# A batched matrix product fed by one stream of DMAs: larger stores, a first load in four pieces, and one loop for all pairs

## The chip, the cores and the metric

The kernel runs on one core of a Trainium2 chip. The metric is the device time of one execution in microseconds (us). The core has five engines that run their own instruction queues and meet at semaphores: TensorE (PE in the profile; its weight loads are PEld) multiplies matrices, VectorE (DVE), ScalarE (ACT) and GpSimd (POOL) work element by element, and SyncE (SP) here does nothing but issue DMAs. Sixteen DMA engines move the data between the memory of the chip (HBM) and the on-chip memory of 128 partitions (SBUF). TensorE writes its results to a small memory of its own (PSUM), from which they have to be copied out.

## The reference

```python
batch, m, k, n = 16, 512, 512, 512
a = np.random.randn(batch, k, m).astype(np.float32)
b = np.random.randn(batch, k, n).astype(np.float32)

def reference(a, b):
    return np.matmul(a.transpose(0, 2, 1), b).astype(np.float32)
```

Sixteen products of 512 x 512 matrices, with a given transposed. Each of a, b and the result is 16.78 MB, so 33.55 MB are read and 16.78 MB written.

## The kernel before

**Pairs of batches.** The batches are taken two at a time, which gives eight pairs. A tile `x` of 128 partitions holds one operand of one pair: batch 0 of the pair lies on partitions 0 to 63 and batch 1 on 64 to 127 (`in_v`, line 34). Each partition has R = 8 successive rows of the matrix, 8 x 2 KB = 16 KB that lie together in HBM. There are four such tiles, `x0` to `x3` (NX = 4), so two pairs fit. Loads are numbered n = 0 to 15: even ones are of a, odd ones of b, and load n goes to tile n % 4.

**The two halves of a pair.** VectorE casts float32 to bfloat16 in two halves of RV = 4 rows (v = 0 and 1), into `abf` and `bbf`, of which there is one tile for each half. TensorE takes half v once both of its casts are there (`s_cast`). One matmul covers the 64 partitions of one batch (g = 0 or 1); the two batches of a pair take turns in the instruction order (lines 140 to 161), each with its own PSUM tiles. The results of a pair add up over both halves; a pair takes 64 matmuls, 32 for each half. ScalarE copies the finished PSUM tiles to the output tile `o` of that pair, in four copies (line 176), and then says so on `s_out` (line 181). There are NO = 7 output tiles for eight pairs, so the last pair reuses that of pair 0 and ScalarE first waits until the store of pair 0 has landed (`s_o0`, line 165).

**The first pair is different.** Its two batches are loaded one after the other, each spread over all 128 partitions (`in0_v`, line 37): a of batch 0, b of batch 0, a of batch 1, b of batch 1, four DMAs of 1 MB with 8 KB for each partition (lines 70 to 73, semaphores `s_f` and `s_x`). VectorE casts them in lines 89 to 98, TensorE has a loop of its own for them with matmuls of the full 128 rows (lines 123 to 139), and ScalarE copies batch by batch (lines 166 to 172). VectorE casts batch 1 into the same tiles as batch 0, so it waits for the matmuls of batch 0 (line 91).

**The queue of DMAs.** SyncE issues everything in one order. From load 4 on it waits until VectorE has cast the tile that is to be overwritten (`s_in`, line 76, counted up by the small memsets of lines 98 and 119). The last load comes in two halves (lines 81 and 82, `s_h`). When the first half of that last load has landed (line 84), SyncE issues the stores, one DMA of 2 MB for each pair, each after its `s_out` (lines 85 to 87). In a store each partition writes 8 KB to each of two batches. So nearly all loads come before all stores in the queue. The store of the last pair stands at the very end, after a barrier (line 188), and GpSimd waits for the other stores (lines 184 to 186).

**Order of the casts.** VectorE's casts of pair i wait for TensorE: half 0 for the matmuls of half 0 of the pair before (`s_v`, line 104; for pair 1 all matmuls of the first pair, line 102), half 1 for all matmuls of the pair before (`s_mm`, line 106). Each also waits for its load (line 112).

Of the kernel before, what the change touches and what calls it, by code (L numbers as in the profile page):

```python
# [8 lines left out]
def kernel(  # L9
# [6 lines left out]
    nc = tc.nc  # L16
    P = 128
    batch, K, M = a.shape
    _, _, N = b.shape
    f32 = mybir.dt.float32  # L20
# [5 lines left out]
    G = 2  # L26
    Q = P // G
    R = K // Q
    V = 2
    RV = R // V  # L30
    T = M // P
    H = T // 2
    pairs = batch // G
    in_v = [x.rearrange("(pair g) (q r) m -> pair (g q) r m", g=G, r=R) for x in (a, b)]


    in0_v = [x.rearrange("batch (p r) m -> batch p r m", r=RV) for x in (a, b)]
    out_v = out.rearrange("(pair g) (c t) n -> pair c g t n", g=G, t=T)

    NX = 4  # L40
    NO = pairs - 1
# [3 lines left out]
    pool = ctx.enter_context(tc.tile_pool(name="sb", bufs=1))  # L45
# [4 lines left out]
    dve_done, act_done = done[:, 0:2 * pairs], done[:, 2 * pairs:3 * pairs]  # L50
    x_ts = [pool.tile([P, R, M], f32, name=f"x{j}") for j in range(NX)]
    abf_ts = [pool.tile([P, RV, M], bf, name=f"abf{v}") for v in range(V)]
    bbf_ts = [pool.tile([P, RV, N], bf, name=f"bbf{v}") for v in range(V)]
    o_ts = [pool.tile([P, G, T, N], f32, name=f"o{j}") for j in range(NO)]
    ps_ts = [[psum.tile([P, 2, N], f32, name=f"ps{g}{h}") for h in range(H)] for g in range(G)]

    s_x = [tc.alloc_semaphore(f"s_x{j}") for j in range(NX)]
    s_f = [tc.alloc_semaphore(f"s_f{j}") for j in range(2)]
    s_h = tc.alloc_semaphore("s_h")
    s_o0 = tc.alloc_semaphore("s_o0")  # L60
    s_o = tc.alloc_semaphore("s_o")
    s_in = tc.alloc_semaphore("s_in")
    s_cast = tc.alloc_semaphore("s_cast")
    s_v = tc.alloc_semaphore("s_v")
    s_mm = tc.alloc_semaphore("s_mm")
    s_ev = [tc.alloc_semaphore(f"s_ev{h}") for h in range(H)]
    s_out = tc.alloc_semaphore("s_out")

    with tc.tile_critical(no_gpsimd_drain=True):  # L69
        for j in range(2):  # L70
            nc.sync.dma_start(x_ts[j][:, 0:RV, :], in0_v[j][0]).then_inc(s_f[j], 16)  # L71
        for j in range(2):
            nc.sync.dma_start(x_ts[j][:, RV:R, :], in0_v[j][1]).then_inc(s_x[j], 16)  # L73
        for n in range(2, 2 * pairs):
            if n >= NX:
                nc.sync.wait_ge(s_in, n - NX + 1)
            src, x = in_v[n % 2][n // 2], x_ts[n % NX]
            if n < 2 * pairs - 1:
                nc.sync.dma_start(x[:], src).then_inc(s_x[n % NX], 16)  # L79
            else:  # L80
                nc.sync.dma_start(x[:, 0:RV, :], src[:, 0:RV, :]).then_inc(s_h, 16)
                nc.sync.dma_start(x[:, RV:R, :], src[:, RV:R, :]).then_inc(s_x[n % NX], 16)

        nc.sync.wait_ge(s_h, 16)
        for i in range(pairs - 1):
            nc.sync.wait_ge(s_out, i + 1)
            nc.sync.dma_start(out_v[i], o_ts[i % NO][:]).then_inc(s_o if i else s_o0, 16)

        for u in range(G):
            if u:  # L90
                nc.vector.wait_ge(s_mm, H)
            for j, bf_ts in enumerate((abf_ts, bbf_ts)):
                nc.vector.wait_ge(s_x[j] if u else s_f[j], 16)
                nc.vector.tensor_copy(  # L94
                    out=bf_ts[0][:], in_=x_ts[j][:, u * RV:(u + 1) * RV, :]
                ).then_inc(s_cast, 1)
                if u == G - 1:
                    nc.vector.memset(dve_done[:, j:j + 1], 0.0).then_inc(s_in, 1)  # L98
        for i in range(1, pairs):
            for v in range(V):  # L100
                if i == 1 and v == 0:
                    nc.vector.wait_ge(s_mm, G * H)
                if i > 1 and v == 0:
                    nc.vector.wait_ge(s_v, G * (i - 1))
                if i > 1 and v == 1:
                    nc.vector.wait_ge(s_mm, G * H * i)
                for n in (2 * i, 2 * i + 1):
                    last = n == 2 * pairs - 1
                    if last and v == 0:
                        nc.vector.wait_ge(s_h, 16)  # L110
                    if last and v == 1 or not last and v == 0:
                        nc.vector.wait_ge(s_x[n % NX], 16 * (n // NX + 1))
                    nc.vector.tensor_copy(  # L113
                        out=(bbf_ts if n % 2 else abf_ts)[v][:],
                        in_=x_ts[n % NX][:, v * RV:(v + 1) * RV, :],
                    ).then_inc(s_cast, 1)
                    if v == V - 1:

                        nc.vector.memset(dve_done[:, n:n + 1], 0.0).then_inc(s_in, 1)  # L119

        for h in range(H):
            nc.tensor.sem_inc(s_ev[h], 1)
        with nc.tensor.Fori(0, G):
            a_m = abf_ts[0][:].rearrange("p r (c t) -> p r t c", t=T)
            nc.tensor.wait_ge(s_cast, 2).then_inc(s_cast, -2)
            for t in range(T):
                h = t // 2
                if t % 2 == 0:
                    nc.tensor.wait_ge(s_ev[h], 1).then_inc(s_ev[h], -1)  # L129
                for r in range(RV):  # L130
                    mm = nc.tensor.matmul(  # L131
                        ps_ts[0][h][:, t % 2, :],
                        a_m[:, r, t],
                        bbf_ts[0][:, r, :],
                        start=(r == 0),
                        stop=(r == RV - 1),
                    )
                if t % 2:
                    mm.then_inc(s_mm, 1)
        with nc.tensor.Fori(0, pairs - 1):  # L140
            for v in range(V):
                nc.tensor.wait_ge(s_cast, 2).then_inc(s_cast, -2)
                for t in range(T):
                    h = t // 2
                    if v == 0 and t % 2 == 0:
                        nc.tensor.wait_ge(s_ev[h], 1).then_inc(s_ev[h], -1)  # L146
                    for r in range(RV):
                        for g in range(G):
                            rows = slice(g * Q, (g + 1) * Q)
                            a_m = abf_ts[v][rows, r, :].rearrange("p (c t) -> p t c", t=T)  # L150
                            mm = nc.tensor.matmul(  # L151
                                ps_ts[g][h][:, t % 2, :],
                                a_m[:, t],
                                bbf_ts[v][rows, r, :],
                                start=(v == 0 and r == 0),
                                stop=(v == V - 1 and r == RV - 1),
                            )
                            if v == 0 and t == T - 1 and r == RV - 1:
                                mm.then_inc(s_v, 1)
                            if v == V - 1 and t % 2 and r == RV - 1:  # L160
                                mm.then_inc(s_mm, 1)

        for i in range(pairs):
            if i == NO:
                nc.scalar.wait_ge(s_o0, 16)
            if i == 0:
                for g in range(G):
                    for h in range(H):
                        nc.scalar.wait_ge(s_mm, H * g + h + 1)
                        nc.scalar.copy(  # L170
                            out=o_ts[0][:, g, 2 * h:2 * h + 2, :], in_=ps_ts[0][h][:]
                        ).then_inc(s_ev[h], 1)
            for h in range(H if i else 0):
                for g in range(G):
                    nc.scalar.wait_ge(s_mm, G * H * i + G * h + g + 1)
                    ev = nc.scalar.copy(  # L176
                        out=o_ts[i % NO][:, g, 2 * h:2 * h + 2, :], in_=ps_ts[g][h][:]
                    )
                ev.then_inc(s_ev[h], 1)

            nc.scalar.memzero(act_done[:, i:i + 1]).then_inc(s_out, 1)  # L181


    with tc.tile_critical(sync_engine=mybir.EngineType.Pool, no_gpsimd_drain=True):
        nc.gpsimd.wait_ge(s_o0, 16)
        nc.gpsimd.wait_ge(s_o, 16 * (pairs - 2))
    tc.no_sync_barrier()
    nc.sync.dma_start(out_v[pairs - 1], o_ts[(pairs - 1) % NO][:])


# [28 lines left out]
```

## Time and profile before

| | |
|---|---|
| median of 10 runs | 123.24 us |
| lowest and highest run | 123.15 and 123.48 us |
| the profiled execution | 123.17 us |
| its span in the profile | 121.4 us |
| instructions | 1207 |
| PE busy | 61.7 us, 51% of the span |
| PEld busy | 34.9 us, 29% |
| DVE busy | 38.1 us, 31% |
| ACT busy | 32.1 us, 26% |
| moved by DMA | 50.33 MB, 415 GB/s over the span |

The span goes from the first to the last instruction of the profile; the remaining 1.8 us of the profiled execution lie around it. All times of single instructions below come from this one execution and are counted from the start of the span. The DMA share is the mean busy share of the 16 DMA engines; it can go a little over 1, since packets are booked where they start and successive ones overlap slightly. "SPq" is the time that an issue of a DMA takes on SyncE's queue, not the transfer itself. A line of the timeline gives the start, the duration, the engine, the line of the kernel, the operation with its tiles, and in brackets how long the engine had been idle and what ended that.

### The profile page before, as it was taken

How to read it: one execution, taken by the hardware profiler on the slowest of the kernel's cores; microseconds unless marked ns; L12 is line 12 of the kernel's file. 1: busy time of each engine (PE TensorE's matmuls, PEld its weight loads, DVE VectorE, ACT ScalarE, POOL GpSimd, SP SyncE). 2: the span in 40 equal slices, each digit the busy share in tenths (PEclk: the TensorE clock that was granted, in tenths of full speed). 3: DMA queues.
4: the chain of work that ended last, by engine and by line, in shares of the span. 5: the costliest groups of instructions: out<-in, count | busy, mean ns of one | idle time of the engine just before them, and what ended most of it. 6: DMA issues, size and time to landing. Idle time of an engine off the chain costs nothing.

```text
span 121.4 us, 1207 instructions
## 1 busy us (share of the span) xinstructions
PE 61.7 (51%) x480; PEld 34.9 (29%) x480; DVE 38.1 (31%) x48; ACT 32.1 (26%) x41; POOL 0.2 (0%) x4
## 2 busy tenths in 40 slices
PE   0007919099379959739979919989900000000000
PEld 0002314066135536424636606655400000000000
DVE  0061070864290394083465447492000000000000
ACT  4000323301900570740092380191560000000000
POOL 0000000000000000000000000000000000000000
PEclk9999999999959999985999999999995555555555
DMA  2999999999999999999999999999999999999994
GB/s 70 429 424 426 443 432 432 432 432 432 432 432 432 432 432 426 426 432 432 432 432 432 432 432 418 426 429 426 426 432 432 424 426 432 424 432 421 429 426 192
DMA packets 4912, 50.33 MB, mean 415 GB/s; under 512 B 432, under 2 KB 432, under 8 KB 432
## 3 DMA queue, kind: packets, MB, share of 16 engines
q1 hardware_dynamic: 4912, 50.33, 97.6%
HBM read 33.55 MB, written 16.78 MB: 415 GB/s over the span
## 4 chain that ended last, share of the span: by engine, by line
DMA 59%; DVE 6%; issue 3%; ACT 3%; SPq 2%; ACTq 0%
DMA x<-in_b_dram 53%; DMA out_dram<-o 6%; ACT o L176 3%; DVE bbf L113 3%; DVE abf L113 3%; SPq L73 1%; SPq L71 1%; SPq L79 0%; DVE done L119 0%; ACTq L69 0%; SPq L214 0%; SPq L69 0%
## 5 line engine op out<-in xcount | busy, mean ns | idle before, releaser
L151 PE MATMUL ps<-bbf,abf 64*128 64x512 bf16 x448 | 52.8, 393 | 13.6 <-PEq L146 13.6
L151 PEld LDWEIGHTS ps<-bbf,abf 64*128 64x128 bf16 x448 | 31.2, 112 | 35.2 <-issue 20.5
L176 ACT COPY o<-ps 128x1024 f32<-128x1024 f32 x28 | 26.3, 1027 | 40.9 <-PE ps L151 36.9
L113 DVE CAST abf<-x 128x2048 bf16<-128x2048 f32 x14 | 17.1, 1224 | 17.4 <-PE ps L151 13.4
L113 DVE CAST bbf<-x 128x2048 bf16<-128x2048 f32 x14 | 17.1, 1225 | 14.6 <-DMA x<-in_b_dram 14.6
L131 PE MATMUL ps<-bbf,abf 128*128 128x512 bf16 x32 | 8.8, 438 | 12.5 <-PEq L129 12.5
L131 PEld LDWEIGHTS ps<-bbf,abf 128*128 128x128 bf16 x32 | 3.7, 121 | 17.1 <-issue 15.1
L170 ACT COPY o<-ps 128x1024 f32<-128x1024 f32 x4 | 4.0, 1012 | 16.1 <-PE ps L131 16.1
L94 DVE CAST abf<-x 128x2048 bf16<-128x2048 f32 x2 | 2.5, 1228 | 11.4 <-DMA x<-in_a_dram 5.8
L94 DVE CAST bbf<-x 128x2048 bf16<-128x2048 f32 x2 | 2.4, 1224 | 1.2 <-DMA x<-in_b_dram 1.2
L181 ACT ACTIVATE done<-done 1x1 uint32<-1x1 uint32 x8 | 1.6, 196 | 0.0
L170 ACT ACT_TABLE_LOAD x1 | 1.3, 1283 | 0.9 <-SPq L69 0.9
L119 DVE MEMSET done<- 1x1 f32 x14 | 0.8, 59 | 0.0
L98 DVE MEMSET done<- 1x1 f32 x2 | 0.1, 59 | 0.0
L203 POOL MEMSET const-bfloat16-1.0<- 128x1 bf16 x1 | 0.1, 101 | 0.0
L203 POOL MEMSET const-uint8-127<- 128x1 uint8 x1 | 0.1, 101 | 0.0
L203 POOL MEMSET const-float32-0.0<- 128x1 f32 x1 | 0.1, 98 | 0.2 <-issue 0.2
L203 POOL MEMSET const-float32-1.0<- 128x1 f32 x1 | 0.1, 98 | 0.0
## 6 DMA issues: line engine op xcount, KB each, us to landing
out_dram<-o SPq DMA_DIRECT2D x8, 2048.0 KB, 21.9
x<-in_a_dram SPq DMA_DIRECT2D x7, 2048.0 KB, 12.2
x<-in_b_dram SPq DMA_DIRECT2D x6, 2048.0 KB, 15.9
x<-in_b_dram SPq DMA_DIRECT2D x4, 1024.0 KB, 12.1
x<-in_a_dram SPq DMA_DIRECT2D x2, 1024.0 KB, 6.8
```

The lines of the kernel that those rows point to most:

```text
L71: nc.sync.dma_start(x_ts[j][:, 0:RV, :], in0_v[j][0]).then_inc(s_f[j], 16)
L73: nc.sync.dma_start(x_ts[j][:, RV:R, :], in0_v[j][1]).then_inc(s_x[j], 16)
L94: nc.vector.tensor_copy(out=bf_ts[0][:], in_=x_ts[j][:, u * RV:(u + 1) * RV, :]).then_inc(s_cast, 1)
L98: nc.vector.memset(dve_done[:, j:j + 1], 0.0).then_inc(s_in, 1)
L113: nc.vector.tensor_copy(out=(bbf_ts if n % 2 else abf_ts)[v][:], in_=x_ts[n % NX][:, v * RV:(v + 1) * RV, :],).then_inc(s_cast, 1)
L119: nc.vector.memset(dve_done[:, n:n + 1], 0.0).then_inc(s_in, 1)
L131: mm = nc.tensor.matmul(ps_ts[0][h][:, t % 2, :], a_m[:, r, t], bbf_ts[0][:, r, :], start=(r == 0), stop=(r == RV - 1),)
L151: mm = nc.tensor.matmul(ps_ts[g][h][:, t % 2, :], a_m[:, t], bbf_ts[v][rows, r, :], start=(v == 0 and r == 0), stop=(v == V - 1 and r == R ...
L170: nc.scalar.copy(out=o_ts[0][:, g, 2 * h:2 * h + 2, :], in_=ps_ts[0][h][:]).then_inc(s_ev[h], 1)
L176: ev = nc.scalar.copy(out=o_ts[i % NO][:, g, 2 * h:2 * h + 2, :], in_=ps_ts[g][h][:])
L181: nc.scalar.memzero(act_done[:, i:i + 1]).then_inc(s_out, 1)
L203: nc = _bacc.Bacc("TRN2", target_bir_lowering=False, num_devices=1)
```

## The change

**Loads.** All pairs now have the layout of `in_v`: two batches side by side on 64 partitions each, in runs of 16 KB for a partition. The separate layout of the first pair goes. The very first load, a of pair 0, is issued in four DMAs: row 0, row 1, rows 2 and 3, rows 4 to 7 of each partition, which are 2, 2, 4 and 8 KB for a partition. The first three count up one semaphore (`s_h[0]`), for which VectorE waits with 48. The load of b of pair 0 is one DMA of 2 MB. The last load keeps its two halves.

**Compute.** The first pair goes through the same casts, the same TensorE loop and the same copies as the others; its own code on VectorE, TensorE and ScalarE goes. The cast of half 0 of pair 1 now waits for `s_v` like that of the later pairs.

**Stores.** The seven output tiles become slices of one tile `o_t`, so that one DMA can take two of them. The first seven pairs are stored in four DMAs: pairs 0 and 1, 2 and 3, 4 and 5 with 4 MB each, and pair 6 with 2 MB. A store waits until both of its pairs are copied. ScalarE's wait for the output tile of pair 0 is therefore a wait for the store of pairs 0 and 1. The store of the last pair is as it was.

```diff
-    in0_v = [x.rearrange("batch (p r) m -> batch p r m", r=RV) for x in (a, b)]
-    out_v = out.rearrange("(pair g) (c t) n -> pair c g t n", g=G, t=T)
+    out_v = out.rearrange("batch (c t) n -> c batch t n", t=T)
...
-    o_ts = [pool.tile([P, G, T, N], f32, name=f"o{j}") for j in range(NO)]
+    o_t = pool.tile([P, NO, G, T, N], f32, name="o")
+    o_ts = [o_t[:, j] for j in range(NO)]
...
-    s_f = [tc.alloc_semaphore(f"s_f{j}") for j in range(2)]
-    s_h = tc.alloc_semaphore("s_h")
+    s_h = [tc.alloc_semaphore(f"s_h{j}") for j in range(2)]
...
-        for j in range(2):
-            nc.sync.dma_start(x_ts[j][:, 0:RV, :], in0_v[j][0]).then_inc(s_f[j], 16)
-        for j in range(2):
-            nc.sync.dma_start(x_ts[j][:, RV:R, :], in0_v[j][1]).then_inc(s_x[j], 16)
-        for n in range(2, 2 * pairs):
+        for n in range(2 * pairs):
             if n >= NX:
                 nc.sync.wait_ge(s_in, n - NX + 1)
-            src, x = in_v[n % 2][n // 2], x_ts[n % NX]
-            if n < 2 * pairs - 1:
-                nc.sync.dma_start(x[:], src).then_inc(s_x[n % NX], 16)
-            else:
-                nc.sync.dma_start(x[:, 0:RV, :], src[:, 0:RV, :]).then_inc(s_h, 16)
-                nc.sync.dma_start(x[:, RV:R, :], src[:, RV:R, :]).then_inc(s_x[n % NX], 16)
+            cuts = (0, 1, 2, RV, R) if n == 0 else (0, RV, R) if n == 2 * pairs - 1 else (0, R)
+            for r0, r1 in zip(cuts, cuts[1:]):
+                done_sem = s_x[n % NX] if r1 == R else s_h[n > 0]
+                nc.sync.dma_start(
+                    x_ts[n % NX][:, r0:r1, :], in_v[n % 2][n // 2][:, r0:r1, :]
+                ).then_inc(done_sem, 16)
 
-        nc.sync.wait_ge(s_h, 16)
-        for i in range(pairs - 1):
-            nc.sync.wait_ge(s_out, i + 1)
-            nc.sync.dma_start(out_v[i], o_ts[i % NO][:]).then_inc(s_o if i else s_o0, 16)
+        nc.sync.wait_ge(s_h[1], 16)
+        for i in range(0, NO, 2):
+            n = min(2, NO - i)
+            nc.sync.wait_ge(s_out, i + n)
+            nc.sync.dma_start(
+                out_v[:, G * i:G * (i + n)],
+                o_t[:, i:i + n].rearrange("p i g t n -> p (i g) t n"),
+            ).then_inc(s_o if i else s_o0, 16)
 
-        for u in range(G):
-            if u:
-                nc.vector.wait_ge(s_mm, H)
-            for j, bf_ts in enumerate((abf_ts, bbf_ts)):
-                nc.vector.wait_ge(s_x[j] if u else s_f[j], 16)
-                nc.vector.tensor_copy(
-                    out=bf_ts[0][:], in_=x_ts[j][:, u * RV:(u + 1) * RV, :]
-                ).then_inc(s_cast, 1)
-                if u == G - 1:
-                    nc.vector.memset(dve_done[:, j:j + 1], 0.0).then_inc(s_in, 1)
-        for i in range(1, pairs):
+        for i in range(pairs):
             for v in range(V):
-                if i == 1 and v == 0:
-                    nc.vector.wait_ge(s_mm, G * H)
-                if i > 1 and v == 0:
-                    nc.vector.wait_ge(s_v, G * (i - 1))
-                if i > 1 and v == 1:
+                if i and v == 0:
+                    nc.vector.wait_ge(s_v, G * i)
+                if i and v == 1:
                     nc.vector.wait_ge(s_mm, G * H * i)
                 for n in (2 * i, 2 * i + 1):
-                    last = n == 2 * pairs - 1
-                    if last and v == 0:
-                        nc.vector.wait_ge(s_h, 16)
-                    if last and v == 1 or not last and v == 0:
+                    split = n in (0, 2 * pairs - 1)
+                    if split and v == 0:
+                        nc.vector.wait_ge(s_h[n > 0], 16 if n else 48)
+                    if split == (v == 1):
                         nc.vector.wait_ge(s_x[n % NX], 16 * (n // NX + 1))
...
-        with nc.tensor.Fori(0, G):
-            a_m = abf_ts[0][:].rearrange("p r (c t) -> p r t c", t=T)
...
-        with nc.tensor.Fori(0, pairs - 1):
+        with nc.tensor.Fori(0, pairs):
...
-            if i == 0:
-                for g in range(G):
-                    for h in range(H):
-                        nc.scalar.wait_ge(s_mm, H * g + h + 1)
-                        nc.scalar.copy(
-                            out=o_ts[0][:, g, 2 * h:2 * h + 2, :], in_=ps_ts[0][h][:]
-                        ).then_inc(s_ev[h], 1)
-            for h in range(H if i else 0):
+            for h in range(H):
...
-        nc.gpsimd.wait_ge(s_o, 16 * (pairs - 2))
+        nc.gpsimd.wait_ge(s_o, 16 * ((NO + 1) // 2 - 1))
     tc.no_sync_barrier()
-    nc.sync.dma_start(out_v[pairs - 1], o_ts[(pairs - 1) % NO][:])
+    nc.sync.dma_start(out_v[:, batch - G:batch], o_ts[(pairs - 1) % NO])
```

More of the change, by code (lines that the diff above doesn't have):

```diff
@@ L122 @@
             nc.tensor.sem_inc(s_ev[h], 1)
-        with nc.tensor.Fori(0, G):
-            a_m = abf_ts[0][:].rearrange("p r (c t) -> p r t c", t=T)
[L125 to L139, printed above, removed]
-        with nc.tensor.Fori(0, pairs - 1):
+        with nc.tensor.Fori(0, pairs):
             for v in range(V):
```

## The prediction

> **What bounds the kernel now.** I read the slice rows of the page first, then its DMA queues, then the table of busy time by stage, then the chain of waits and the timeline. The slice rows and the queue row:
>
> ```profile
> PE   0007919099379959739979919989900000000000
> DMA  2999999999999999999999999999999999999994
> GB/s 70 429 424 426 443 432 432 432 432 432 432 432 432 432 432 426 426 432 432 432 432 432 432 432 418 426 429 426 426 432 432 424 426 432 424 432 421 429 426 192
> q1 hardware_dynamic: 4912, 50.33, 97.6%
> ```
>
> The DMA engines are busy in every slice but the first and the last; TensorE (PE) has whole slices of nothing, and none from slice 30 on. So the program is one stream of 50.33 MB through 16 DMA engines: 33.55 MB of loads, then 16.78 MB of stores. Three things can change its time: the time per row moved, a hole in the stream, and its two ends. The stages, in the busy time by stage (the last two columns are the DMA share and GB/s):
>
> ```profile
> 1.80:2.00 0.20, 0.00 (x0) 0.00 (x0) 0.00 (x0) 0.20 (x1) 0.00 (x0) 1.00 0.54 205
> 2.00:2.20 0.20, 0.00 (x0) 0.00 (x0) 0.00 (x0) 0.18 (x1) 0.00 (x0) 1.00 0.31 123
> 2.20:2.40 0.20, 0.00 (x0) 0.00 (x0) 0.00 (x0) 0.00 (x0) 0.00 (x0) 1.00 1.66 328
> 2.40:2.60 0.20, 0.00 (x0) 0.00 (x0) 0.00 (x0) 0.00 (x0) 0.00 (x0) 1.00 0.00 0
> 2.60:2.80 0.20, 0.00 (x0) 0.00 (x0) 0.00 (x0) 0.00 (x0) 0.00 (x0) 1.00 0.80 205
> 2.80:3.00 0.20, 0.00 (x0) 0.00 (x0) 0.00 (x0) 0.00 (x0) 0.00 (x0) 1.00 0.62 205
> ...
> 20.00:72.00 52.00, 39.82 (x327) 22.98 (x324) 25.37 (x32) 20.33 (x27) 0.00 (x0) 0.93 1.01 433
> ...
> 92.00:118.00 26.00, 0.00 (x0) 0.00 (x0) 0.00 (x0) 0.00 (x0) 0.00 (x0) 0.50 1.01 429
> ```
>
> Loads of 16 KB rows run at 433 GB/s, stores of 8 KB rows at 429, both at a DMA share of 1.01: no hole to fill. Only the ramp is loose: bytes start at 1.8 us, and no packet starts from 2.4 to 2.6. From 1.8 to 3.4 (3.0 to 3.4 shows 369 and 410) the rates times 0.2 us give 369 KB where 430 GB/s would give 688: 0.74 us lost. The issues on the SyncE queue (SPq) at the start and at the change from loads to stores, and the waits that tie the other engines to the stream:
>
> ```profile
> 0.94 0.39 SPq L71 DMA_DIRECT2D x<-in_a_dram  x1
> 1.39 0.42 SPq L71 DMA_DIRECT2D x<-in_b_dram  x1
> 1.86 0.42 SPq L73 DMA_DIRECT2D x<-in_a_dram  x1
> 2.33 0.72 SPq L73 DMA_DIRECT2D x<-in_b_dram  x1
> ...
> 22.86 1.23 DVE L113 CAST bbf<-x 128x2048 bf16<-128x2048 f32 x1 [0.29 <-DMA x<-in_b_dram]
> ...
> 25.28 0.33 SPq L79 DMA_DIRECT2D x<-in_a_dram  x1
> ```
>
> ```profile
> 78.80 7.41 DMA out_dram<-o
> 86.23 3.76 ACT o L176 x4
> ```
>
> An issue takes some 0.42 us, the fourth 0.72. The second pair's last load has landed at 22.86, and the load into the first pair's buffer of a (load 6, counted from 0) is issued at 25.28 once that buffer is cast. The first store is asked for at 78.80, when half of the last load (1 MB, 2.4 us) is still to come, and lands 7.41 us later; ScalarE (ACT) waits for it, copies the last pair out in 3.76 us, and the last store joins a queue that is busy to 120 us. The page's chain gives DMA 59% and no engine more than 6%.
>
> **What the Trainium skill says.** "DMA: Bandwidth & Descriptors", section "Anatomy of one DMA — SWDGE (gpsimd) path": the semaphore write at the end of a DMA costs about one cycle, and most of the fixed 2 us of a DMA is completion latency. It is stated for another issue path than SyncE's, but the trace agrees as far as it goes: 2 MB stores queued behind each other keep 429 GB/s, so a boundary between queued DMAs costs nothing visible, and fewer of them win nothing. The same page, "Latency and other measured facts", puts the first byte of such a DMA at about 600 ns; here the first bytes appear between 1.8 and 2.0, 0.5 to 0.7 us after the first issue ends at 1.33. It also warns that HBM rows at a large power-of-two pitch slow DMAs down; the stores here already step 1 MB from batch to batch at 429 GB/s, so the trace shows no such loss. "SBUF — State Buffer", section "The DMA setup-cost knee (why "@ 1 MiB" ≠ asymptote)", has a 256 KiB transfer at 224 GB/s alone; that is a bound for the small first pieces if they do not overlap, and no row of this trace shows such a size.
>
> **The change, part by part.**
>
> 1. *Price of a row.* 16 engines at 433 GB/s give 605 ns per 16 KB row, at 429 they give 305.5 ns per 8 KB row. Twice the second less the first: about 5.6 ns per row whatever its length (3 to 9, as the rates are whole GB/s), and 37.5 ns per KB. A 2 KB row then costs 80.6 ns, a 4 KB row 155.5 ns: estimates from these two rates.
>
> 2. *First load in four.* Each engine has 8 of the 128 partitions. The first half of a was 8 rows of 8 KB; it becomes 8 of 2, 8 of 2 and 8 of 4 KB: 16 more rows, 16 x 5.6 = +0.09 us. The second half stays at 8 KB.
>
> 3. *b of the first pair.* Two DMAs of 8 KB rows become one of 16 KB rows: 8 rows fewer per engine, -0.045 us.
>
> 4. *Stores.* Seven DMAs become four (two pairs, two, two, one) beside the last, with the same 8 KB rows; loads go from 19 to 20 DMAs, so 27 become 25: two completion writes fewer per engine, between 0 and 0.01 us, taken as 0.
>
> 5. *Hand-over between the small pieces.* A 256 KB piece gives an engine 8 x 80.6 = 0.645 us of work. SyncE issues every 0.45 us, fast enough. But the descriptors come at a slower rate: the fourth issue was held to 0.72 us, and the stores of 256 rows took a median of 1.30 us each, 0.65 us per 128 rows. So the next piece arrives 0 to 0.08 us after the last is used up, twice: I take 0.02 each, +0.04 us. If the stall at 2.4 us stays it gives the descriptors time to get ahead and even this goes. Bounds: below, the shorter rows take the stall away, -0.74 us at the very most; above, each restart costs a new start. At the page's 224 GB/s, 256 KB takes 1.17 us in place of 0.61, so 0.56 us each, +1.1 us at most.
>
> 6. *Later start of the compute.* The first matmul needs half of a and all of b: 4 MB (4.19 million bytes) landed, 9.69 us at 433 before the 22.86 of the 8 MB mark: 13.2 us, and matmuls at 14.7 (24.39 less 9.69) in place of 9.77. Lines 94, 131 and 170 go; the first pair now takes the path of the others, with 64 half-height matmuls. A pair takes 7.1 us (24.39 to 31.49), plus 1.6 us while the clock is cold (16 matmuls took 5.21 us first, 3.62 then): done at 23.4, against 24.01, when the second half of the next pair's a is cast. Load 4 waits for the second cast of a: 25.28 - 9.69 = 15.6 us, earlier than the 16.30 of before, with 4 MB still queued until 22.9. Load 6 is issued at about 25.3 as now, and the queue has work until 32.5. VectorE's new wait for the first half of TensorE's loop is met at 14.7 + 3.6 + 1.6 = 19.9, before that cast's 21.34 of now. Cost 0; the cover is 7 us of queued loads. From the second pair on everything follows the landings, which are the same.
>
> 7. *Stores of 4 MB and the last pair.* ACT's wait for the first store ends 4.9 us later, at 91.1; copies to 94.9; last store asked for at 95.1. The stores before it occupy the engines to about 115 (120.0 less 4.9). Cover 20 us, cost 0. SyncE's waits for two evictions per store come last for pair 6, alone in the fourth store: its copies start at 78.45 and take 3.76, so 82.3, while 12 MB of earlier stores keep the engines busy.
>
> 8. *First 4 MB store.* It has 512 rows to describe, 2.6 us at 0.65 per 128, and 2.4 us of load as cover. The start of the kernel shows that engines begin on the first descriptors while the others are made: starts at 1.8 to 2.0, and the rest at 2.2 to 2.4. So half of the engines get work early, the other half after some 2.0 us (1.0 us for the first 64 rows, as at the start, and three more lots of 64 at 0.32): 80.8 against 81.2. Cost 0. If nothing starts before all 512 are made, it is 1.0 + 7 x 0.32 = 3.3 us, 82.1: a hole of 0.85 us.
>
> 9. *Tail.* The last store has the same 256 rows and its wait is as before: 0.
>
> Sum: 0.09 - 0.045 + 0.04 = +0.085 us. The profiled execution took 123.17 us itself (span 121.4 and 1.8 around it), 0.07 below the median; 123.17 + 0.085 = 123.26 there, 123.32 on the median of 123.24. I forecast 123.3.
>
> **Rivals.**
>
> *Faster:* small first rows shorten the ramp. For it: the empty 0.2 us at 2.4, and the trouble lies where 8 KB rows of all engines begin together. Against: it comes 0.5 us after the first bytes on all engines at once, as if it were not a matter of row length. Half of the 0.74 us, after the +0.045 of rows: 122.9.
>
> *Slower, first pieces:* the engines run dry at the two hand-overs and start again, as in 5. It decides from 0.13 us of hole each (0.25 in all). For it: 0.645 us of work against 0.65 of descriptors leaves no reserve. Against: the stall gives one. With 0.25 each, half of the bound: 123.24 + 0.045 + 0.5 = 123.8.
>
> *Slower, first big store:* part 8's hole, 123.3 + 0.85 = 124.1 at worst, deciding from 0.25. Against: the stepped start at 1.8 us.
>
> *Slower, store rate:* four batches at 1 MB pitch in one DMA run 1% below 429 GB/s: 34 us of stores, +0.34, 123.65. Against: each engine still writes 8 KB rows one after another, as now.
>
> That the change does not do what it says is no rival: the orders of the two programs show the four first loads and the four stores.
>
> **How the numbers follow.** This kernel's measurement tells 0.2% (0.25 us) from no change at best. Forecast, within that: 0.50. Faster 0.17. First pieces 0.19, big store 0.09, rate and anything else 0.05: slower 0.33. Range 122.8 to 124.1: it takes in the faster case, the pieces and the hole of part 8; the likeliest case alone lies in 123.1 to 123.5.
>
> **What would show it.** Right: DMA packets 4912 + 16 x (16 - 8 - 2) = 5008, share of 1.01 at 433 and 429 GB/s in the same stages, matmuls from about 14.7, load 4 at about 15.6, last store asked for near 95, span 121.3 to 121.7. Wrong: under 369 KB moved between 1.8 and 3.4 us (pieces), or well over it (faster); a share under 0.95 between 81 and 83 (big store); under 427 GB/s from 92 to 118 (rate); a load issued when the queue has run dry before 35 us (part 6).

## The result and the profile after

The changed kernel takes 124.95 us (median of 9 runs, 124.47 to 125.89) against 123.24: a ratio of 1.0139, 95% interval 1.0124 to 1.0154. It is slower by 1.7 us, and outside the forecast's range of 122.8 to 124.1. The profiled execution took 124.46 us with a span of 122.5 us, which is 1.29 us and 1.1 us over those of the kernel before, so the traces show most of the loss, and some later runs lost more.

First the slice rows and the queue row of the page of the changed kernel:

```profile
DMA  2999999999999999999999999999999999999993
GB/s 82 310 448 428 417 428 433 433 428 439 428 428 439 433 444 433 433 433 428 428 428 428 428 433 415 415 428 428 428 425 431 428 431 425 431 428 428 425 431 147
DMA packets 5008, 50.33 MB, mean 411 GB/s; under 512 B 400, under 2 KB 400, under 8 KB 784
q1 hardware_dynamic: 5008, 50.33, 97.3%
```

The packets are the 5008 that were counted out in the forecast, and from the third slice on the rates are close to those of before (415 to 448 GB/s up to the last slice, 418 to 443 before). The second slice (3.1 to 6.1 us) shows 310 GB/s, where before had 429. The DMA row alone hides it: its digit is 9 in both. The busy time by stage of the changed kernel (the last two columns are the DMA share and GB/s):

```profile
1.80:3.00 1.20, 0.00 (x0) 0.00 (x0) 0.00 (x0) 0.38 (x1) 0.00 (x0) 1.00 0.67 203
3.00:4.00 1.00, 0.00 (x0) 0.00 (x0) 0.00 (x0) 0.00 (x0) 0.00 (x0) 1.00 0.78 250
4.00:5.00 1.00, 0.00 (x0) 0.00 (x0) 0.00 (x0) 0.00 (x0) 0.00 (x0) 1.00 1.00 307
5.00:6.00 1.00, 0.00 (x0) 0.00 (x0) 0.00 (x0) 0.00 (x0) 0.00 (x0) 1.00 1.06 334
...
20.00:34.00 14.00, 12.53 (x110) 7.12 (x106) 6.30 (x8) 6.65 (x9) 0.00 (x0) 1.00 1.01 431
...
40.00:60.00 20.00, 16.23 (x137) 9.15 (x134) 9.66 (x13) 7.64 (x10) 0.00 (x0) 0.91 1.01 433
100.00:118.00 18.00, 0.00 (x0) 0.00 (x0) 0.00 (x0) 0.00 (x0) 0.00 (x0) 0.50 1.01 427
...
120.00:121.00 1.00, 0.00 (x0) 0.00 (x0) 0.00 (x0) 0.00 (x0) 0.00 (x0) 0.50 0.49 205
```

The same four stages of the kernel before:

```profile
1.80:3.00 1.20, 0.00 (x0) 0.00 (x0) 0.00 (x0) 0.38 (x1) 0.00 (x0) 1.00 0.65 177
3.00:4.00 1.00, 0.00 (x0) 0.00 (x0) 0.00 (x0) 0.00 (x0) 0.00 (x0) 1.00 0.96 401
4.00:5.00 1.00, 0.00 (x0) 0.00 (x0) 0.00 (x0) 0.00 (x0) 0.00 (x0) 1.00 1.01 426
5.00:6.00 1.00, 0.00 (x0) 0.00 (x0) 0.18 (x1) 0.00 (x0) 0.00 (x0) 1.00 1.04 434
```

From 1.8 to 6.0 us the changed kernel moves 1.2 x 203 + 250 + 307 + 334 = 1135 KB, the kernel before 1473 KB by the same sum. The 338 KB less are 0.79 us at 430 GB/s. Two things are to be seen. From 3 to 4 us the DMA share is 0.78: engines stand idle. From 4 to 6 us it is 1.0 and more, and still only 307 and 334 GB/s move: the engines count as busy, and some of the rows take longer. Of the 128 rows of 4 KB in the third piece, 79 took 159 ns and 48 took 164 to 531 ns; in e4 (below), where the same piece is moved after 70 us, all 128 took 159 ns. The rest of the loss is unevenness. The marks with which the 16 engines report the end of one DMA lie 0.54 to 0.66 us apart in the trace of before. In that of the changed kernel they lie 1.0 to 1.2 us apart, from the end of the first load to the last store. The program ends with its slowest engine. At the last store the slowest mark comes 0.27 us behind the mean of the 16 before and 0.58 us after: 0.3 us more. With the 0.79 us that makes the 1.1 us by which the spans differ.

The timeline of the changed kernel shows the rest of the forecast's steps:

```profile
0.94 1.82 SPq L75 DMA_DIRECT2D x<-in_a_dram  x4
2.80 0.43 SPq L75 DMA_DIRECT2D x<-in_b_dram  x1
3.27 0.50 SPq L75 DMA_DIRECT2D x<-in_a_dram  x1
3.81 0.45 SPq L75 DMA_DIRECT2D x<-in_b_dram  x1
...
15.83 9.49 PE L121 MATMUL ps<-bbf,abf 64*128 64x512 bf16 x64 [15.83 <-PEq L116]
...
16.72 0.33 SPq L75 DMA_DIRECT2D x<-in_a_dram  x1
...
25.37 1.23 DVE L100 CAST abf<-x 128x2048 bf16<-128x2048 f32 x1
...
79.93 8.57 SPq L83 DMA_DIRECT2D out_dram<-o  x4
96.19 0.37 SPq L151 DMA_DIRECT2D out_dram<-o  x1
```

Matmuls start at 15.83 (forecast 14.7), load 4 is issued at 16.72 (15.6), the first store is asked for at 79.93 (78.80 before) and the last at 96.19 (95.1). All are about 1.1 us late, because the data are; none has made a hole: the stages from 20 to 34 and from 40 to 60 us keep 431 and 433 GB/s, the stores 427.

### The profile page after: what moved, and what is told of

The parts are those of the page before. It is cut to its first block, busy times and chain, and to the rows that moved or that the text cites. A ratio compares the mean times of both kernels' runs of the same rounds, so it can differ in the third digit from the quotient of the medians.

```text
span 122.5 us, 1263 instructions
## 1 busy us (share of the span) xinstructions
PE 62.6 (51%) x512; PEld 36.0 (29%) x512; DVE 38.1 (31%) x48; ACT 31.8 (26%) x41; POOL 0.2 (0%) x4
## 2 busy tenths in 40 slices
DMA packets 5008, 50.33 MB, mean 411 GB/s; under 512 B 400, under 2 KB 400, under 8 KB 784
## 3 DMA queue, kind: packets, MB, share of 16 engines
q1 hardware_dynamic: 5008, 50.33, 97.3%
## 4 chain that ended last, share of the span: by engine, by line
DMA 47%; PE 8%; DVE 5%; issue 3%; ACT 2%; ACTq 1%
DMA x<-in_b_dram 37%; DMA out_dram<-o 10%; PE ps L121 8%; DVE abf L100 3%; ACT o L139 2%; DVE bbf L100 2%; ACTq L66 1%; DVE done L106 0%; ACT done L144 0%
## 5 line engine op out<-in xcount | busy, mean ns | idle before, releaser
L121 PE MATMUL ps<-bbf,abf 64*128 64x512 bf16 x512 | 62.6, 402 | 26.2 <-PEq L116 26.2
L121 PEld LDWEIGHTS ps<-bbf,abf 64*128 64x128 bf16 x512 | 36.0, 114 | 52.3 <-issue 36.4
```

Source lines behind the costliest of these rows:

```text
L121: mm = nc.tensor.matmul(ps_ts[g][h][:, t % 2, :], a_m[:, t], bbf_ts[v][rows, r, :], start=(v == 0 and r == 0), stop=(v == V - 1 and r == R ...
```

## The experiments

Every run is timed beside runs of the kernel before on the same chip. In the diffs below, the semaphores that the pieces count up and the counts that the casts wait for follow the number of pieces and are not shown; other lines left out are marked by dots. The ratio with its 95% interval is what to compare; 0.1% is 0.12 us.

| run | what differs | median us | ratio to before |
|---|---|---|---|
| changed kernel | | 124.95 | 1.0139 (1.0124 to 1.0154) |
| e1 | first load in one DMA | 123.67 | 1.0033 (1.0021 to 1.0045) |
| e2 | first load in two halves | 123.63 | 1.0031 (1.0021 to 1.0042) |
| e3 | kernel before, its first DMA in three pieces | 124.36 | 1.0097 (1.0081 to 1.0112) |
| e4 | pieces on load 14 | 123.75 | 1.0037 (1.0025 to 1.0049) |
| e5 | pieces from neighbouring addresses | 125.20 | 1.0179 (1.0153 to 1.0206) |
| e6 | first half of the load as one DMA of 2 KB rows | 123.90 | 1.0048 (1.0034 to 1.0062) |
| e7 | first pair from the old addresses | 123.41 | 1.0017 (1.0010 to 1.0024) |
| e8 | kernel before with 4 MB stores | 123.25 | 1.0003 (0.9994 to 1.0011) |
| e9 | first load in four equal pieces | 124.58 | 1.0097 (1.0082 to 1.0113) |
| e10 | one small piece at the head | 124.01 | 1.0050 (1.0037 to 1.0064) |
| e11 | old addresses in the old order | 123.39 | 1.0006 (0.9998 to 1.0015) |
| e12 | kernel before, second DMA from ScalarE's queue | 123.40 | 1.0009 (1.0000 to 1.0017) |
| e13 | 1 MB ahead of the small pieces | 124.39 | 1.0086 (1.0072 to 1.0100) |
| e14 | first load in eight pieces | 125.60 | 1.0187 (1.0174 to 1.0201) |
| e15 | pieces on load 1 | 124.12 | 1.0072 (1.0058 to 1.0086) |
| e16 | pieces on load 2 | 124.15 | 1.0069 (1.0056 to 1.0082) |
| e17 | kernel before, first four DMAs merged into two | 125.14 | 1.0149 (1.0135 to 1.0164) |
| e18 | pieces on load 4 | 123.87 | 1.0051 (1.0036 to 1.0065) |

### Are the pieces the cause, and is anything else?

e1 and e2 undo the pieces:

```diff
-            cuts = (0, 1, 2, RV, R) if n == 0 else (0, RV, R) if n == 2 * pairs - 1 else (0, R)
+            cuts = (0, RV, R) if n == 2 * pairs - 1 else (0, R)           # e1
+            cuts = (0, RV, R) if n in (0, 2 * pairs - 1) else (0, R)      # e2
```

> The changed kernel with its very first load in one DMA of 16 KB rows; all else as changed. If the four pieces are the cause (short rows, or hand-over between small DMAs): 123.0 to 123.5 us, the loss gone. If the later start of the compute, the single loop or the 4 MB stores cost the time: still above 124.3.

> The changed kernel with its first load in two DMAs of 8 KB rows, a pitch of 16 KB. Short rows as the cause: 8 KB rows ran at full rate elsewhere, so 123.1 to 123.5. If a DMA boundary in the first microseconds costs by itself, a third of the loss stays: about 123.8. If the cause is elsewhere: above 124.3.

Both leave 0.3% and take away 1.1%: the pieces cost some 1.3 us. The remaining 0.3% was in neither expectation. One DMA of 2 MB and two of 1 MB do not differ. e3 does the opposite and cuts only the first DMA of the kernel before:

```diff
-            nc.sync.dma_start(x_ts[j][:, 0:RV, :], in0_v[j][0]).then_inc(s_f[j], 16)
+            cuts = (0, RV) if j else (0, 1, 2, RV)
+            for r0, r1 in zip(cuts, cuts[1:]):
+                nc.sync.dma_start(x_ts[j][:, r0:r1, :], in0_v[j][0][:, r0:r1, :]).then_inc(s_f[j], 16)
```

> The kernel before, with only its first DMA (half of a, 8 KB rows at a pitch of 8 KB) cut into rows 0, 1 and 2-3. If the hand-over of small DMAs at the start costs the time: the whole loss, 124.6 to 125.2. If it is short rows at a large pitch (2 KB of each 16 KB touch an eighth of the addresses, here a quarter): about half, 123.7 to 124.3. If the rest of the change costs it: 123.2 to 123.4.

1.0097: the pieces alone cost the kernel before 1.2 us, with the old layout, stores and loops. The median of 124.36 us lies just above the range named for half of the loss, and below the one for the whole.

The stores and the layout were then taken one at a time. e8 is the kernel before with only the stores of the change (the diff of lines 85 to 87, of the tile `o_t` and of the waits):

> The kernel before with nothing but the change of the stores (4 MB per DMA, two pairs each). If the stores cost nothing, as forecast: 123.1 to 123.4. If they make up the 0.35 us that stay without the pieces: 123.5 to 123.8.

1.0003: the stores cost nothing, as forecast. e7 and e11 keep the change but load the first pair without pieces and from the old addresses, in the order a, a, b, b (e7) and in the old order a, b, a, b (e11, whose loop is shown; `in0_v` is that of before):

```diff
+        for v in range(V):
+            for n in range(2):
+                nc.sync.dma_start(
+                    x_ts[n][:, v * RV:(v + 1) * RV, :], in0_v[n][v]
+                ).then_inc(s_h[0] if n == v == 0 else s_x[n], 16)
+        for n in range(2, 2 * pairs):
...
```

> The changed kernel without pieces, its first two loads read from the addresses of before (1 MB each, rows of 8 KB that follow each other, one batch over all partitions), in the order a, a, b, b; the products of the first pair are other ones. If the 0.35 us that stay without the pieces come from the layout of the first loads: 123.1 to 123.4. If they come from the stores or the compute: 123.5 to 123.8.

> As the kernel with the old addresses, with the first four DMAs in the order of before too (a, b, a, b): loads as before to the byte, compute and stores as changed; the products of the first pair are other ones. If the last 0.2 us lie in the order of the first loads: 123.1 to 123.35. If they lie in the later compute or the single loop: 123.35 to 123.5.

e11 has the loads of before and the stores and compute of the change, and stands at 1.0006, its interval apart from that of e2 (1.0021 to 1.0042). Its median of 123.39 us falls into the range named for the later compute, but the kernel before took 123.31 us on the same chip, so the ratio decides. The new layout of the first two loads costs 0.25%, 0.3 us, and the later compute in a single loop nothing that can be measured. With the 1.3 us of the pieces that is the loss of 1.7 us, but for 0.1. How the 0.3 us divide between addresses (e7) and order (e11) is not settled, since the intervals of e7 and e11 overlap.

### Short rows, addresses, or the number of DMAs?

The pieces differ from one DMA in three ways: their rows are short, they pick 2 KB out of each 16 KB, and they are more DMAs. e5 keeps the DMAs and their sizes but takes each piece from one closed stretch of memory:

```diff
+    a_near = a.rearrange("batch (r p) m -> batch p r m", r=RV)
+    a_rows = a.rearrange("batch (p r) m -> batch p r m", r=RV)
...
+                if n == 0:
+                    src = a_near[0][:, r0:r1, :] if r1 < R else a_rows[1]
```

> The changed kernel; the pieces of the first load are taken from batch 0 with the partitions 2 KB apart in HBM instead of 16 KB, so that each piece is one closed stretch, and the second half from batch 1 (8 KB apart). The DMAs and their bytes stay; only addresses change, and the products of the first pair are other ones. If the 16 KB pitch of short rows makes the start slow: 123.3 to 123.8. If it is small DMAs handed over at the start: 124.5 to 125.2, as the changed kernel.

1.0179: nothing is won, it is rather slower, though its interval still touches that of the changed kernel. Sparse addresses are not the cause. (The third piece here has rows of 2 KB in place of 4 KB, because its two rows no longer lie together.) e6 loads the first 1 MB as rows of 2 KB in a single DMA:

```diff
+            cuts = (0, RV, R) if n in (0, 2 * pairs - 1) else (0, R)
...
+                if n == 0 and r0 == 0:
+                    src = in_v[0][0][:, 0:R:2, :]
```

> The changed kernel; the first half of the first load is one DMA of 512 rows of 2 KB (every second row of the tile's eight) in place of three DMAs, so the products of the first pair are other ones. If the number of small DMAs at the start costs the time: 123.5 to 123.9, as with two halves. If it is short rows while the queue is being filled: 124.3 to 125.3.

1.0048 against 1.0031 for two halves, with intervals that overlap: 512 short rows in one DMA cost some 0.2 us, if anything, where the three DMAs cost 1.3. The busy time by stage of e6, from an execution of 124.42 us, the longest of its five:

```profile
1.80:3.00 1.20, 0.00 (x0) 0.00 (x0) 0.00 (x0) 0.38 (x1) 0.00 (x0) 1.00 0.44 126
3.00:4.00 1.00, 0.00 (x0) 0.00 (x0) 0.00 (x0) 0.00 (x0) 0.00 (x0) 1.00 1.07 412
4.00:5.00 1.00, 0.00 (x0) 0.00 (x0) 0.00 (x0) 0.00 (x0) 0.00 (x0) 1.00 1.02 389
```

The same short rows begin more slowly (126 GB/s against 203 up to 3 us), and then move at 412 and 389 GB/s, where the pieces moved at 250 and 307. What is left is the number of DMAs, or their size: in a load of 2 MB more DMAs are also smaller ones, and no run tells the two apart. The forecast's own mechanism, that an engine uses up a piece of 0.64 us before the next descriptors come at 0.65, was put to the test by larger pieces (e9) and by a single hand-over (e10):

```diff
+            cuts = (0, 2, RV, 6, R) if n == 0 else (0, RV, R) if n == 2 * pairs - 1 else (0, R)   # e9
+            cuts = (0, 1, RV, R) if n == 0 else (0, RV, R) if n == 2 * pairs - 1 else (0, R)      # e10
```

> The changed kernel with its first load in four equal DMAs of 512 KB (4 KB rows). Each gives an engine 1.24 us of work, about twice the 0.65 us in which descriptors for 128 rows were delivered. If engines run dry because the next descriptors come late: nothing to run dry, 123.5 to 123.9. If each extra DMA at the start costs a fixed time: two more than with two halves, 124.4 to 125.0.

> The changed kernel with its first load in three DMAs, of 256 KB, 768 KB and 1 MB: one hand-over from a piece that lasts 0.64 us, in place of two. If late descriptors make the loss: about half of it, 123.9 to 124.5. If it takes all four pieces or the shorter rows of several of them: 123.5 to 123.9.

e9 stands at 1.0097: pieces that last 1.24 us, about twice as long as descriptors take, still cost 0.8 us over two halves, as its expectation had it for a price of each extra DMA. Descriptors that come at the forecast's rate of 0.65 us for each DMA do not explain that. A slower delivery at the start is not excluded, but within one DMA it was not slower: the 412 GB/s of e6 are 201 rows of 2 KB in a microsecond, 128 in 0.64 us. The busy time by stage of e9:

```profile
3.00:3.60 0.60, 0.00 (x0) 0.00 (x0) 0.00 (x0) 0.00 (x0) 0.00 (x0) 1.00 0.74 198
3.60:4.20 0.60, 0.00 (x0) 0.00 (x0) 0.00 (x0) 0.00 (x0) 0.00 (x0) 1.00 0.79 225
4.20:5.40 1.20, 0.00 (x0) 0.00 (x0) 0.00 (x0) 0.00 (x0) 0.00 (x0) 1.00 0.97 393
5.40:6.60 1.20, 0.00 (x0) 0.00 (x0) 0.12 (x1) 0.00 (x0) 0.00 (x0) 1.00 1.06 345
```

Idle shares and slow rows appear here too, the latter as late as 5.4 to 6.6 us, at full share. One more DMA (e10) costs 0.2 us over e2, with intervals that just overlap. Its 124.01 us lie in the range named for late descriptors, but 0.2 of 1.3 us is far from the half that they were to make. Two more cost 0.7 (e13, below), 0.8 (e9) and 1.3 (the changed kernel). e14 cuts the load into eight:

```diff
+            cuts = range(R + 1) if n == 0 else (0, RV, R) if n == 2 * pairs - 1 else (0, R)
```

> The changed kernel with its first load in eight DMAs of 256 KB. If each extra DMA costs 0.4 to 0.65 us: six more than with two halves, 126.0 to 127.5. If descriptors come at 0.65 us per DMA and that alone holds the engines: 8 x 0.65 = 5.2 us for 2 MB that need 4.9, so 124.0 to 124.6; if the loss saturates after the first two hand-overs: 124.8 to 125.5.

1.0187: six more DMAs than two halves cost 1.9 us, 0.3 each. So there is no fixed price for a DMA: 0.2 in e10, 0.3 here, 0.4 in e9 and 0.65 in the changed kernel. The loss neither stops after two hand-overs nor grows as fast as the first expectation said.

### Where in the stream do small DMAs cost?

The same pieces were moved: behind 1 MB of the same load (e13), and to loads 1, 2, 4 and 14 (e15, e16, e18, e4).

```diff
+            cuts = (0, RV, 5, 6, R) if n == 0 else (0, RV, R) if n == 2 * pairs - 1 else (0, R)       # e13
+            cuts = (0, 1, 2, RV, R) if n == 1 else (0, RV, R) if n == 2 * pairs - 1 else (0, R)       # e15; e16 and e18 with 2 and 4
+            cuts = (0, 1, 2, RV, R) if n == 2 * pairs - 2 else (0, RV, R) if n == 2 * pairs - 1 else (0, R)   # e4
```

> The changed kernel with the same four DMAs of the first load in the order 1 MB, 256 KB, 256 KB, 512 KB: 2.4 us of work stand ahead of the small ones. If the cost comes from small DMAs at the head of an empty queue: 123.5 to 124.0. If every extra DMA in the first burst costs 0.4 to 0.65 us: 124.4 to 125.0.

> The changed kernel with the four pieces on load 1 (b of the first pair), behind 2 MB that take 4.9 us; to be compared with one DMA per load, 123.67. If the distance from the first bytes decides: 123.7 to 124.0. If every extra DMA in the first burst costs 0.4 us or more: 124.3 to 124.9.

> The changed kernel with the four pieces on load 2 (a of the second pair), behind 4 MB that take 9.7 us. If the distance from the first bytes decides: 123.6 to 123.8, as with the pieces on load 14. If every extra DMA in the first burst costs 0.4 us or more: 124.3 to 124.9.

> The changed kernel with the four pieces on load 4, issued after the first burst at about 16 us and moved at 22 to 27 us. If membership of the first burst is what costs 0.45 us: 123.6 to 123.85, as with load 14. If the place in the run hardly matters and a full queue does not hide it: 124.0 to 124.3.

> The changed kernel with the four pieces moved from the first load to the last load of a (load 14), where the queue is full. If short rows at a pitch of 16 KB are read slowly wherever they are: 0.6 to 1.7 us over 123.2, so 123.8 to 124.9. If the loss belongs to the start (engines that run dry or start cold): 123.1 to 123.5.

Measured against one DMA per load (e1, 1.0033), the pieces cost 0.5 us on load 1, 0.4 on load 2, and 0.2 on load 4 and 0.05 on load 14, where the intervals overlap with that of e1. At the head they cost 1.3 us, behind 1 MB 0.7 us (both against e2). So the price falls with the distance from the first bytes, in steps that neither expectation had: not gone behind 2 or 4 MB, and within the noise once the first four loads are through. A single execution can still show a dip there: in the profiled execution of e4, which took 124.15 us, the longest of its six, the pieces show:

```profile
66.00:70.00 4.00, 4.00 (x30) 2.31 (x28) 0.91 (x1) 0.00 (x0) 0.00 (x0) 0.72 1.03 442
70.00:73.00 3.00, 2.50 (x24) 1.36 (x20) 1.44 (x2) 2.22 (x3) 0.00 (x0) 1.00 0.92 339
73.00:77.00 4.00, 3.60 (x34) 2.45 (x36) 2.38 (x5) 1.60 (x3) 0.00 (x0) 1.00 1.04 436
```

And e13, whose small pieces come after 5 us, behind 1 MB:

```profile
5.00:6.00 1.00, 0.00 (x0) 0.00 (x0) 0.00 (x0) 0.00 (x0) 0.00 (x0) 1.00 0.93 283
6.00:7.00 1.00, 0.00 (x0) 0.00 (x0) 0.87 (x1) 0.00 (x0) 0.00 (x0) 1.00 0.81 215
7.00:8.00 1.00, 0.00 (x0) 0.00 (x0) 0.36 (x1) 0.00 (x0) 0.00 (x0) 1.00 1.06 424
```

The dip sits where the two pieces of 256 KB are moved (their rows start at 4.98 to 7.65 us), not at a fixed time.

### Can the start be made faster than before?

Two tries on the kernel before. e12 issues its second DMA from ScalarE's queue, beside the first:

```diff
-            nc.sync.dma_start(x_ts[j][:, 0:RV, :], in0_v[j][0]).then_inc(s_f[j], 16)
+            (nc.scalar if j else nc.sync).dma_start(x_ts[j][:, 0:RV, :], in0_v[j][0]).then_inc(s_f[j], 16)
```

> The kernel before with its second DMA (half of b, 1 MB) issued from ScalarE's queue at the start. If the start of the stream is limited by how fast one queue's descriptors come: 122.7 to 123.1, faster than before. If the stall near 2.4 us comes from elsewhere: 123.1 to 123.5.

1.0009: no gain, and the stall is not cured by a second queue: the trace of e12 shows 0 GB/s from 2.2 to 2.4 us and 41 up to 2.6. e17 merges the first four DMAs into two:

```diff
-    in0_v = [x.rearrange("batch (p r) m -> batch p r m", r=RV) for x in (a, b)]
+    in0_v = [x.rearrange("batch (p r) m -> p batch r m", r=RV) for x in (a, b)]
...
-            nc.sync.dma_start(x_ts[j][:, 0:RV, :], in0_v[j][0]).then_inc(s_f[j], 16)
-        for j in range(2):
-            nc.sync.dma_start(x_ts[j][:, RV:R, :], in0_v[j][1]).then_inc(s_x[j], 16)
+            nc.sync.dma_start(
+                x_ts[j][:].rearrange("p (g r) m -> p g r m", g=G), in0_v[j][:, 0:G]
+            ).then_inc(s_x[j], 16)
```

> The kernel before with its first four DMAs of 1 MB merged into two of 2 MB, the same rows from the same addresses. If each DMA in the first burst costs some 0.4 us: 122.5 to 123.0. If only small or short-rowed DMAs cost: 123.1 to 123.5.

1.0149, slower by 1.8 us, for a reason that neither line had. The profiled execution of e17 took 127.3 us where the others took 125.0 to 125.3, so its order of events is used, and not the size of its times. The second batch of a and the issue of load 4 in its timeline:

```profile
20.84 1.23 DVE L94 CAST abf<-x 128x2048 bf16<-128x2048 f32 x1 [6.34 <-PE ps L131]
...
22.12 0.33 SPq L79 DMA_DIRECT2D x<-in_a_dram  x1
```

and its busy time by stage:

```profile
20.00:24.00 4.00, 1.29 (x6) 0.47 (x5) 2.38 (x4) 1.01 (x1) 0.00 (x0) 0.89 0.89 291
24.00:30.00 6.00, 4.59 (x16) 1.73 (x14) 1.38 (x2) 2.12 (x3) 0.00 (x0) 0.79 0.93 390
```

The kernel before computes the two batches of the first pair one after the other through the same cast tiles. With all of a ahead of b, batch 0 starts 5 us later, batch 1 waits for it, and load 4 is issued at 22.12 in place of 16.30. The first four loads are then nearly all moved (the fourth is reported as landed at 22.97), and the stream has a hole. e17 therefore says nothing on the number of DMAs. It does show what the order a, b, a, b is good for in the kernel before. The single loop of the change, which casts both batches at once and issues load 4 at 16.72, does not need it: e7, in the order a, a, b, b, stands at 1.0017.

## Why the prediction was wrong

- **What bounds the kernel** held: one stream, whose rates in the middle (433 and 427 to 429 GB/s) did not change, and whose two ends decide. So did the price of a row (part 1): it was worked out from loads of 16 KB rows and stores of 8 KB rows, and the packets of the two traces show 611 ns for the first and 309 ns for 8 KB rows of loads and stores alike, so 7 ns per row in place of 5.6; most rows of 4 and 2 KB took 159 and 84 ns, against 155.5 and 80.6. The packet count held, and so did the stores in their outcome (parts 4, 7 and 8: e8 at 1.0003, a DMA share of 1.00 from 81 to 83 us) and the tail. The step of 1 MB in the stores is no test of the warning that the forecast took from the Trainium skill ("DMA: Bandwidth & Descriptors", section "Latency and other measured facts"): the pitch measured there is from partition to partition, and that is 8 KB in these stores.
- **Later start of the compute** (part 6) held in its outcome, with less room than worked out. The first pair was to be done at 23.4 against 24.01; it was done at 25.32, and the next cast began at 25.37, right behind it. Of the 1.9 us, 1.1 came from the late data and 0.8 from matmuls that took 9.49 us in place of 8.7. The queue covered it, as the 7 us of loads were to: 431 GB/s from 20 to 34 us, and e11 at 1.0006.
- **Hand-over between the small pieces** (part 5) is the step that failed. It was taken at +0.04 us with an upper bound of 1.1; e1, e2 and e3 put it at 1.2 to 1.3. Its mechanism failed with it: descriptors that come 0.65 us apart behind 0.64 us of work would have spared pieces of 1.24 us, and e9 shows that they were not spared. The DMA share below 1 from 3 to 4 us shows some idling. Over the four stages up to 6 us the engines are busy for 3.64 us against 3.79 before, so idling makes 0.15 of the 0.79 us. The rest is rows that take longer while the engines count as busy, and the 0.3 us beside it is engines that end up further apart.
- **The sign** that the forecast named for slow pieces, less than 369 KB moved between 1.8 and 3.4 us, came true with 313 KB, but it tells nothing: e8 and e11, which lose no time, moved 336 and 312 KB in it. The difference lies after 3.4 us: 316 GB/s up to 6 us against 425.
- **b of the first pair** (part 3) counted rows only, -0.045 us. The layout of the first two loads cost 0.3 us (e2 against e11), a term that the sum did not have.
- **The range.** The rival of the first pieces was the right one, but it was priced at half of its bound (123.8), with a chance of 0.19. Its full bound would have given 124.4, and 124.7 with the layout's 0.3 us, still short of 124.95. The bound was an estimate from the 224 GB/s of a 256 KiB transfer in the Trainium skill ("SBUF — State Buffer", section "The DMA setup-cost knee (why "@ 1 MiB" ≠ asymptote)"), used twice; the third piece, of 512 KB, was priced at its row rate and was among the slow ones (307 and 334 GB/s from 4 to 6 us).
- **The stall at 2.4 us** was read as cover for the descriptors. In the changed kernel it did not come there: 317 GB/s moved from 2.4 to 2.6 us, where no packet started in the kernel before. Its low stood at 2.8 to 3.2 us with 118 GB/s, and the pieces stayed slow up to 6 us.

What stays open is why some rows of small DMAs take longer at the start; no view shows what a busy engine waits for. It is shown that it isn't sparse addresses (e5), short rows as such (e6) or descriptors that come 0.65 us apart (e9), that it grows with the number of DMAs, which here are also smaller (e9, e10, e14), and that it fades with the distance from the first bytes (e15, e16, e18, e4).

## What to carry to other kernels

In this kernel, one saturated stream of DMAs, the start was the loose part, and there an extra DMA cost 0.2 to 0.7 us (256 to 768 KB each), although its eight more rows per engine are worth 0.05 in the middle of the stream. Start such a stream with few DMAs of 1 MB or more, and cut only loads that come late: 4 MB queued ahead did not suffice (e16, 0.4 us), while on loads 4 and 14 the price was within the noise. Before merging loads, look at which cast frees the first buffer: e17 lost 1.8 us because a reload came 6 us later.

## What the runs showed of the hardware that was not expected

- A busy DMA share can hide a slow stream: 1.00 and 1.06 with 307 and 334 GB/s. The share tells idling, the GB/s column tells the rest.
- Unevenness between the 16 engines that arises in the first microseconds can stay to the end: 1.1 us at the first load and 1.0 us at the last store of the changed kernel, 0.6 and 0.6 before. Pieces are not needed for it, and it can shrink: in e1, which loads first in one DMA, it was 1.0 and then 0.8 us.
- The Trainium skill, "DMA: Bandwidth & Descriptors", section "Bandwidth", advises DMAs of at least 1 MiB for 75% of the peak rate, by measurements of DMAs that GpSimd issued. No run here measures that share, but at the head of the stream the runs agree in direction (e2 against e9 and e14), and far from the start the loss was too small to tell from the noise (e4, 0.05 us).
- The runs of the changed kernel spread over 1.4 us (124.47 to 125.89), those of the kernel before over 0.4. Whether the start makes that spread isn't shown: the runs of e14, with eight pieces, spread over 0.2 (125.46 to 125.66).
